# Pooling stage of a hybrid encoder trunk: loads a block ahead, and the next stages' weights in between

## The chip, the cores and the metric

The kernel runs on one core of a Trainium2 chip. Its time is the device time of one execution in microseconds (us); three runs of the kernel before gave 2900.6, 2905.15 and 2907.33 us, median 2905.15. The engines are named as in the profile: PE (TensorE matmul), DVE (VectorE), ACT (ScalarE), POOL (GpSimd), and SP, on which nearly all DMAs of this kernel are issued.

## The reference, cut to what matters

One layer: a combined input projection of x (4096 tokens, width 1024) feeds four mixers of width 256, whose outputs are merged by an output projection.

```python
z = x @ w_in                       # one projection for all four mixers, N_COLS columns
def pool_mix(u, w_grp, scale):     # the mixer of the stage that is changed
    cs = cumsum(u)                 # along the tokens
    means = [(cs[t] - cs[t - win]) / min(t + 1, win) for win in (2, 4, 8, 16)]
    d = concat(means) - u          # 64 columns for each window
    return einsum('bsgc,gcd->bsgd', d, w_grp) * scale   # then gated by silu of a further 256 columns
# retention_mix, mlstm_mix, rwkv7_mix: the stages that follow, each with its columns of w_in
out = layer_norm(alpha * x + concat(mixers) @ w_out + gated_embedding)
```

Products run on operands that are split exactly in two parts (hi, the cast, and lo, the rest), with three matmuls for each pair: hi·hi, hi·lo and lo·hi.

## The kernel before, in words

Tokens are worked on in 16 blocks of 256. The stages follow each other: pooling (`pooling`), retention, the matrix memory (mLSTM), and at last RWKV with the output. `pooling` goes through the blocks: `dense(b)` loads the block's x in four quarters of the contraction (`load_x`, `fetch`: a DMA into a raw tile L83, the cast to hi on ACT L84, the subtraction for lo on DVE L85), then runs 48 matmuls into `zu` (the pooled columns) and 24 for each half of the tokens into `zpg` (the gate, with 8 columns of mLSTM gates). `mix(b - 1)` makes the windows' sums on POOL (`s`, L784 to L789), the differences on DVE (`dp`, L798), a small product on PE (`yp`, L803), and the result `Yp` on DVE and POOL (L805, L806), stored by SP (L729).

In between the stage prepares right operands for the next two stages, which use seven products in place of eight, so that four of their seven weight operands are sums of quarters of the weights. `sums(name, k)` loads four pieces of a row k (L1288) into tiles `w0` to `w3`, makes four subtractions on POOL (L1290) and stores them as `T5`, `T7`, `T6`, `T4` in DRAM (L1291); `right(name, n)` loads an operand (L1310), casts it (L1311) and subtracts (L1312). Each of the four rows of `w_rt` (retention), six operands of retention and four rows of `w_ml` (mLSTM) is one entry of a list; one entry is taken per block, from block 2 on.

What sets the order on the engines: the program is written in this order and then ordered by a scheduler with a simulated time line; an instruction wrapped in `keep_in_program_order` stays in the order of the program among those so wrapped. Every engine, and SP's queue too, runs its instructions in the order they stand in. Buffers are rings: x parts `xh` and `xl` have 5 (`XB`), raw tiles 3 (and up to 12 early loads take a tile of another ring, `spare`), `w0` to `w3` one each. Retention's first tiles are the x quarters `xr` (L1347) and their hi parts `Ah` (L1336); the pools of the pooling stage are closed before, so `xr` may stand where `w0` to `w3` stood.

```python
for _ in range(1 if i < self.NB else len(todo)):
    if todo and i >= 2:
        todo.pop(0)()
```

Of the kernel before, what the change touches and what calls it, by code (L numbers as in the profile page):

```python
# [9 lines left out]
F32 = mybir.dt.float32  # L10
# [7 lines left out]
P = 128  # L18
# [3 lines left out]
XB = 5  # L22
SOON = 800
H = D // 2
PLAIN = 5
# [17 lines left out]
class Trunk:  # L43
# [27 lines left out]
    def fetch(self, hi, lo, src, nm, eng):  # L71
        """load float32 data and split it exactly into hi + lo"""
# [3 lines left out]
        if self.spare % 2:  # L76
            raw = self.zp.tile([P, 2, 15 + TB], F32, name=f"raw{nm}", tag="z2")[:, :, 0:G]
        else:
            raw = self.xp.tile([P, 2, G], F32, name=f"raw{nm}", tag="raw", bufs=3)
# [7 lines left out]
    def weights(self, name, g0, w=G, pool=None, bufs=5, gates=False):  # L87
        """hi and lo parts of columns g0..g0+w of a weight matrix"""
# [6 lines left out]
        def parts():  # L95
            for k in range(0, KT, 2):
                ks = slice(k, k + 2)
                yield self.fetch(hi[:, ks, :w], lo[:, ks, :w], self.a[name][:, ks, g0:g0 + w], f"{name}_{g0}_{k}",
                                 nc.vector if k < 4 else nc.gpsimd)
            if gates:  # L100
                yield self.fetch(hi[:, :, G:], lo[:, :, G:], self.a[name][:, :, g0 + w:g0 + w + 8], f"{name}_g",
                                 nc.gpsimd)
        return (hi, lo), parts()

    def lazy(self, *args, **kw):
        """a weight group that is loaded where it is first used"""
# [11 lines left out]
    def load_x(self, b, more=None, between=None):  # L118
        """the block's tokens in quarters of the contraction; three of eight come from the pool more"""
        his, los = [], []  # L120
        for k in range(0, KT, 2):
            p, n = (more, 3) if more is not None and (4 * b + k // 2) % 8 in (1, 4, 7) else (self.xp, XB)
# [16 lines left out]
    def dense(self, jobs, nk=KT, apart=False):  # L139
        """out = lhsT.T @ rhs for each job; operands are (hi, lo) by contraction tile.  # L140
        The jobs share one bank unless apart and advance together, so one start flag clears it."""
# [7 lines left out]
    def dense_k(self, jobs):  # L149
        """the same in steps of one contraction tile, in this order on the engine"""  # L150
# [8 lines left out]
    def cols(self, z, w, x, n=2):  # L159
        """columns of one weight group on the partitions, tokens along the row"""  # L160
# [3 lines left out]
    def toks(self, jobs, nk=KT, apart=False):  # L164
        """tokens on the partitions: jobs of (out, weights, x, first token)"""
# [4 lines left out]
    def silu_gate(self, sg, z):  # L170
        """twice z * sigmoid(z)"""
# [13 lines left out]
    # ------------------------------------------------------------------ RWKV  # L185
# [6 lines left out]
    def _rwkv_out(self, es):  # L192
# [20 lines left out]
        # low-rank weights: decay rows (hi, lo), rate rows (lo, hi), against twice the upper part of their input  # L213
# [43 lines left out]
        def mixed(b, out, z, c0, n):  # L257
            """z + (previous token's z - z) * mu, by columns"""
# [11 lines left out]
        # what a block goes through, in pieces: generators that yield the time of the products they have issued  # L270
# [53 lines left out]
        def l(b):  # L324
            # low-rank decay and rate
# [32 lines left out]
        def n(b):  # L358
            # squared norm of the removal key, by tokens in the order of the rows of its products
# [11 lines left out]
            # rows (kappa, beta) of an even chunk, (beta, kappa) of an odd one  # L371
# [61 lines left out]
        def s_(b, cc):  # L433
            # token-major copies of (kappa, beta)
# [11 lines left out]
        def p_(b, cc):  # L446
            # scores of the chunk
# [52 lines left out]
        # inverse of I - N, N strictly upper in this layout  # L500
# [23 lines left out]
        def iv(b):  # L524
# [3 lines left out]
            with self.soon():  # L528
                # the four blocks of 4 on the diagonal, row by row from below
# [7 lines left out]
                # pairs of blocks: X12 = X11 (N12 X22), the inner product where N has zeros  # L537
# [25 lines left out]
        def pt(b):  # L563
            # pairs of 16 to blocks of 32: rows and columns of one block of 32, what N has in the pairs meets zeros
# [29 lines left out]
        def pu(b):  # L594
            # blocks of 32 to 64
# [23 lines left out]
        def chain(b):  # L619
            """the four chunks of a block, one after another; yields where their products wait"""  # L620
# [90 lines left out]
    def head_norm(self, pool, Y, eps, nm):  # L711
        """normalise each 64-wide head of Y [P, 2, 256] in place"""
# [18 lines left out]
    # ------------------------------------------------------------------ pooling  # L731
    def pooling(self, es):
# [6 lines left out]
        p2 = pool("p2", bufs=2)  # L739
        self.mm = pool("pmm", bufs=4, space=PSUM)  # L740
# [4 lines left out]
        # the first products wait for these alone  # L745
# [12 lines left out]
        bl = {}  # L758

        def dense(b):  # L760
            x = self.load_x(b) if b else x0
# [13 lines left out]
        def mix(b):  # L775
# [25 lines left out]
            for c in range(2):  # L801
                for i in range(2):
# [7 lines left out]
        todo = [lambda k=k: self.sums(ws, "w_rt", k) for k in range(4)]  # L810
        qpair = lambda nm: [self.aq.tile([P, 4, H], F32R, name=f"{nm}{g}", tag="q") for g in range(2)]
        todo += [lambda n=n: self.rtB.update({n: self.right("w_rt", n, (self.wpair if n in (1, 5, 2, 6) else qpair)(f"rB{n}"),
                                                           lambda nm: ws.tile([P, H], F32, name=nm, tag=f"w{nm[-1]}"))})
                 for n in (1, 5, 2, 6, 4, 7)]
        todo += [lambda k=k: self.sums(ws, "w_ml", k) for k in range(4)]
        for i in range(self.NB + 1):
            if i < self.NB:
                dense(i)
            if i >= 1:
                mix(i - 1)  # L820
            for _ in range(1 if i < self.NB else len(todo)):
                if todo and i >= 2:
                    todo.pop(0)()

    # ------------------------------------------------------------------ retention
# [133 lines left out]
    # ------------------------------------------------------------------ mLSTM  # L959
    def gates(self, cp, es0):  # L960
        """the stabiliser and the decays of every chunk of 128 tokens, rows (chunk, head)"""
# [724 lines left out]
```

## Time and profile before

| | before |
|---|---|
| runs | 2900.6, 2905.15, 2907.33 us |
| profiled execution, first to last instruction | 2898.2 us |
| PE busy | 2773.1 us (96%), 21940 matmuls |
| DVE busy | 2270.0 us (78%) |
| POOL, ACT busy | 1156.9 us (40%), 974.5 us (34%) |
| mean granted TensorE clock | 0.974 of full speed |
| DMA queue q1 | 277.46 MB, 30.5% of 16 engines' span |

The profiled execution is 2898.2 us from its first to its last instruction; the runs, which include what lies around that, are 2.4 to 9.1 us longer. Times in rows are microseconds from the start of the span unless marked ns. A busy PE is not PE at its peak: the ends of matmuls are modelled and overlap. A row of idle time names what ended it.

### The profile page before, as it was taken

To read this page: it belongs to the slowest core of one execution; us is meant where nothing else is said; L and a number is where in the kernel's file an instruction comes from. 1 tells how busy PE (TensorE), PEld (TensorE's weight loads), DVE (VectorE), ACT (ScalarE), POOL (GpSimd) and SP (SyncE) were. 2 spreads that over 40 slices of the span, in tenths; PEclk is the share of its full clock that TensorE was granted. 3 is DMA by queue.
4 is the path that set the end of the run, shared out by engine and by line. 5 is a ranking of instruction groups with operands and counts; after the bars stand their busy time and mean duration, and the time that the engine had idled before them with its cause. 6 is when DMAs were issued, how large, how long until landed. Compare 5 with 4: busy or idle time off the path is not lost.

```text
span 2898.2 us, 57364 instructions
## 1 busy us (share of the span) xinstructions
PE 2773.1 (96%) x21940; PEld 2466.1 (85%) x21940; DVE 2270.0 (78%) x5639; ACT 974.5 (34%) x2100; POOL 1156.9 (40%) x1231
## 2 busy tenths in 40 slices
PE   7899999999999999798999999999999999999997
PEld 7898888878999999688999999998998788777885
DVE  5657788887999999976777777778847566689997
ACT  3423223234433333333333333334423233432221
POOL 6654555553333333421232333223326111156665
PEclk9899999999999999888999999999999999999998
DMA  7743222223211111321111111112437444643441
GB/s 241 218 142 102 59 66 66 63 72 110 71 59 56 59 53 55 103 59 29 47 34 41 44 37 45 34 45 60 133 106 260 149 139 138 221 153 139 148 157 66
DMA packets 250499, 281.13 MB, mean 97 GB/s; under 512 B 69488, under 2 KB 166512, under 8 KB 250224
## 3 DMA queue, kind: packets, MB, share of 16 engines
q1 hardware_dynamic: 250224, 277.46, 30.5%
q8 instruction: 172, 2.82, 0.4%
q14 instruction: 103, 0.84, 0.1%
HBM read 209.69 MB, written 67.70 MB: 96 GB/s over the span
## 4 chain that ended last, share of the span: by engine, by line
PE 41%; DVE 10%; POOL 3%; DMA 2%; issue 2%; ACT 1%; SPq 0%; POOLq 0%; DVEq 0%; ACTq 0%
PE ry L273 3%; PE gp L273 2%; DVE ro L1578 2%; DVE ro L1557 1%; PE sa L273 1%; PE l L273 1%; PE zg L154 1%; DVE ro L1560 1%; PE zpl L147 1%; PE zpl L145 1%; PE zpl L146 1%; PE zg L155 1%; PE zg L156 1%; POOL ro L1561 1%; PE zpe L145 1%
## 5 line engine op out<-in xcount | busy, mean ns | idle before, releaser
L1336 ACT CAST Ah<-xr 128x512 fp32r<-128x512 f32 x189 | 117.0, 620 | 277.7 <-PE zrb L1372 58.7
L1337 DVE TENSOR_TENSOR Al<-xr,Ah 128x512 fp32r<-128x512 f32 x135 | 99.8, 739 | 76.5 <-ACT Ah L1336 75.7
L677 POOL TENSOR_TENSOR SAV<-SAV,bon 64x256 f32<-64x256 f32 x64 | 40.7, 636 | 283.9 <-PE ry L273 282.3
L85 DVE TENSOR_TENSOR xl<-rawx,xh 128x512 fp32r<-128x512 f32 x148 | 120.9, 821 | 39.8 <-ACT xh L84 38.9
L145 PE MATMUL zqk<-xh,wh_w_ml 128*128 128x256 f32 x512 | 149.1, 291 | 1.1 <-ACT xh L1078 1.1
L146 PE MATMUL zqk<-xl,wh_w_ml 128*128 128x256 f32 x512 | 149.1, 291 | 0.3 <-DVE xl L1079 0.3
L147 PE MATMUL zqk<-xh,wl_w_ml 128*128 128x256 f32 x512 | 149.2, 291 | 0.0
L84 ACT CAST xh<-rawx 128x512 fp32r<-128x512 f32 x148 | 91.6, 619 | 168.8 <-DMA rawx<-in_xT 72.3
L1337 POOL TENSOR_TENSOR Al<-xr,Ah 128x512 fp32r<-128x512 f32 x54 | 71.8, 1330 | 135.7 <-ACT Ah L1336 72.2
L1561 POOL TENSOR_TENSOR ro<-ro,ln_b 128x512 f32<-128x512 f32 x64 | 100.6, 1591 | 53.9 <-DVE ro L1560 53.9
L660 DVE SCALAR_TENSOR_TENSOR S<-ds,eC,Se 64x64 f32<-64x64 f32 x256 | 72.5, 283 | 53.4 <-PE ds L273 48.7
L866 POOL TENSOR_TENSOR rot<-rot,sw 128x256 f32<-128x256 f32 x64 | 69.4, 1085 | 94.2 <-DVE sw L865 88.5
L145 PEld LDWEIGHTS zqk<-xh,wh_w_ml 128*128 128x128 f32 x512 | 98.0, 191 | 3.6 <-ACT xh L1078 1.6
L147 PEld LDWEIGHTS zqk<-xh,wl_w_ml 128*128 128x128 f32 x512 | 98.1, 192 | 2.4
L146 PEld LDWEIGHTS zqk<-xl,wh_w_ml 128*128 128x128 f32 x512 | 98.2, 192 | 2.0 <-DVE xl L1079 0.8
L459 DVE SCALAR_TENSOR_TENSOR g<-gp,rc,c_rmask 128x128 f32<-128x128 f32 x256 | 72.1, 343 | 33.9 <-PE gp L273 32.8
L145 PE MATMUL zu<-xh,wh_w_pl 128*128 128x256 f32 x256 | 78.7, 308 | 14.7 <-ACT xh L84 8.9
L1356 POOL TENSOR_TENSOR xr<-xr,xr 128x512 f32<-128x512 f32 x27 | 35.5, 1316 | 141.8 <-DVE xr L1353 141.7
L146 PE MATMUL zu<-xl,wh_w_pl 128*128 128x256 f32 x256 | 78.2, 305 | 12.0 <-DVE xl L85 12.0
L1185 DVE SCALAR_TENSOR_TENSOR xc<-zc,c_convw,xc 128x256 f32<-128x256 f32 x192 | 86.2, 497 | 0.4
L273 PE MATMUL ry<-SAV,g 64*64 64x64 f32 (+1 forms) x1024 | 83.5, 223 | 0.0
L798 DVE SCALAR_TENSOR_TENSOR dp<-s,c_pinv,us 64x256 f32<-64x256 f32 (+1 forms) x64 | 44.5, 695 | 47.9 <-POOL s L784 41.7
(1120 smaller groups left out, 10675.9 us busy)
## 6 DMA issues: line engine op xcount, KB each, us to landing
rawx<-in_xT SPq DMA_DIRECT2D x148, 256.0 KB, 3.3
xr<-in_xT SPq DMA_DIRECT2D x108, 256.0 KB, 2.9
mr<-in_xT SPq DMA_DIRECT2D x64, 256.0 KB, 3.1
rp<-in_x SPq DMA_DIRECT2D x64, 256.0 KB, 3.1
s<-rp SPq DMA_DIRECT2D x64, 256.0 KB, 2.5
yo<-y SPq DMA_DIRECT2D x16, 1024.0 KB, 4.9
ro<-s SPq DMA_DIRECT2D x16, 1024.0 KB, 5.0
out<-ro SPq DMA_DIRECT2D x32, 512.0 KB, 2.6
```

The costliest lines, as they stand in the source:

```text
L84: nc.scalar.copy(out=hi, in_=raw)
L85: eng.tensor_tensor(out=lo, in0=raw, in1=hi.bitcast(F32), op=ALU.subtract)
L145: nc.tensor.matmul(out, lh(k), rh(k), start=(k == 0 and (apart or i == 0)), stop=False, skip_group_check=True)
L146: nc.tensor.matmul(out, lh(k), rl(k), start=False, stop=False, skip_group_check=True)
L147: nc.tensor.matmul(out, ll(k), rh(k), start=False, stop=(k == nk - 1), skip_group_check=True)
L273: mm = lambda *args, **kw: keep(nc.tensor.matmul(*args, **kw))
L459: V.scalar_tensor_tensor(out=g1[cc][:, hh, p, e], in0=gp[hh][:, p, e], scalar=rc[:, cc, e, i:i + 1], in1=msk[:, 64 * e:64 * e + P], op0=AL ...
L660: V.scalar_tensor_tensor(out=Sn[hv, p, hv], in0=ds[hv, p], scalar=eC[hv, p, c:c + 1], in1=Se[hv, p], op0=ALU.mult, op1=ALU.add)
L1185: V.scalar_tensor_tensor(out=xc[:, t], in0=zc[t // 2][:, t % 2, j:j + TB], scalar=cw[:, t, j:j + 1], in1=xc[:, t], op0=ALU.mult, op1=ALU.add)
L1336: self.nc.scalar.copy(out=hi, in_=src)
L1337: eng.tensor_tensor(out=lo, in0=src, in1=hi.bitcast(F32), op=ALU.subtract)
L1561: Q.tensor_tensor(out=rg, in0=rg, in1=ln["ln_b", g], op=ALU.add)
```

## The change

Five things change. In the loop of `pooling`, the loads of block i + 1 are written ahead of `dense(i)` (before: at the start of `dense(b)`). The x parts get two more buffers (pool `px`), so seven quarters in all. The four rows of sums of `w_rt` are written at the ends of blocks 1 to 5, the six operands at blocks 6 to 11, the sums of `w_ml` at blocks 12 to 16; of a row, the loads and subtractions stand at one block and the four stores at the next one, just ahead of the next row's loads. The DMAs of sums and operands, and the operands' casts, are kept in program order. And of the gate weights, the 8 gate columns are loaded first, and all of their lo parts are made on DVE.

```diff
 def fetch(self, hi, lo, src, nm, eng):
-        if self.spare % 2:
+        if self.spare % 2 and list(src.shape) == [P, 2, G]:
...
 def weights(...):
         def parts():
+            if gates:
+                yield self.fetch(hi[:, :, G:], lo[:, :, G:], self.a[name][:, :, g0 + w:g0 + w + 8], f"{name}_g",
+                                 nc.vector)
             for k in range(0, KT, 2):
...
-                                 nc.vector if k < 4 else nc.gpsimd)
-            if gates:
-                yield self.fetch(hi[:, :, G:], lo[:, :, G:], self.a[name][:, :, g0 + w:g0 + w + 8], f"{name}_g",
-                                 nc.gpsimd)
+                                 nc.vector if k < 4 or gates else nc.gpsimd)
...
 def load_x(self, b, more=None, between=None):
-            p, n = (more, 3) if more is not None and (4 * b + k // 2) % 8 in (1, 4, 7) else (self.xp, XB)
+            p, n = (more, 2) if more is not None and (4 * b + k // 2) % 7 in (3, 6) else (self.xp, XB)
...
 def pooling(self, es):
+        px = pool("px", bufs=2)
...
+        xs = {0: x0}
         def dense(b):
-            x = self.load_x(b) if b else x0
+            x = xs.pop(b)
...
-        todo = [lambda k=k: self.sums(ws, "w_rt", k) for k in range(4)]
-        todo += [...the six operands of w_rt, by right()...]
-        todo += [lambda k=k: self.sums(ws, "w_ml", k) for k in range(4)]
+        keep = tc.keep_in_program_order
+        def operand(n):
+            t = (self.wpair if n in (1, 5, 2, 6) else qpair)(f"rB{n}")
+            self.rtB[n] = self.right("w_rt", n, t, lambda nm: ws.tile([P, H], F32, name=nm, tag=f"w{nm[-1]}"), keep)
+        def rows(name):
+            for k in range(4):
+                part = self.sums(ws, name, k, keep=keep)
+                next(part)
+                yield
+                next(part, None)
+        plan = {i: [] for i in range(self.NB + 1)}
+        for i in range(5):
+            plan[1 + i].append("rt")
+            plan[12 + i].append("ml")
+        for i, n in enumerate((1, 5, 2, 6, 4, 7)):
+            plan[6 + i].append(n)
+        row = {nm: rows(f"w_{nm}") for nm in ("rt", "ml")}
         for i in range(self.NB + 1):
+            if i + 1 < self.NB:
+                xs[i + 1] = self.load_x(i + 1, more=px)
             if i < self.NB:
                 dense(i)
             if i >= 1:
                 mix(i - 1)
-            for _ in range(1 if i < self.NB else len(todo)):
-                if todo and i >= 2:
-                    todo.pop(0)()
+            for w in plan[i]:
+                if w in row:
+                    next(row[w], None)
+                else:
+                    operand(w)
...
 def sums(self, ws, name, k, j=0, w=H, keep=lambda i: i):
-            nc.sync.dma_start(out=t[i], in_=self.a[name][:, 4 * kh + k, o:o + n])
+            keep(nc.sync.dma_start(out=t[i], in_=self.a[name][:, 4 * kh + k, o:o + n]))
         for i, o, x, y in ((5, 1, 0, 1), (7, 0, 3, 0), (6, 3, 3, 1), (4, 2, 2, 3)):
             Q.tensor_tensor(out=t[o], in0=t[x], in1=t[y], op=ALU.subtract)
-            nc.sync.dma_start(out=self.T[name][i][:, k, j:j + n], in_=t[o])
+        yield
+        for i, o in ((5, 1), (7, 0), (6, 3), (4, 2)):
+            keep(nc.sync.dma_start(out=self.T[name][i][:, k, j:j + n], in_=t[o]))
```

SP's queue in the middle of the stage, before: `rawx3_0` is the first quarter of block 3's x, `w..._rt30` and `T..._rt` are loads and stores of sums of `w_rt`, `y0` the store of block 0.

```order
L83 DMA rawx3_6_674<-in_xT 128x512
L1288 DMA w0w_rt30_1157<-in_w_rt 128x512
L729 DMA y0_72<-Yp0_475 128x2x256
L1291 DMA T6w_rt_636<-w3w_rt20_984 128x512
L1288 DMA w1w_rt30_1151<-in_w_rt 128x512
L1291 DMA T4w_rt_634<-w2w_rt20_982 128x512
```

And now, at the store of block 1:

```order
L83 DMA rawx5_0_866<-in_xT 128x512
L83 DMA rawx5_2_872<-in_xT 128x512
L729 DMA y1_73<-Yp1_673 128x2x256
L1316 DMA T5w_rt_507<-w1w_rt00_510 128x512
...
L1316 DMA T4w_rt_506<-w2w_rt00_512 128x512
L1311 DMA w1w_rt10_681<-in_w_rt 128x512
```

The store of block 0 stood behind the loads of block 3, that of block 1 now stands behind half of block 5's; the sums' transfers, which stood between single quarters of x, now stand together behind the store of a block.

SP's queue before, where the sums of `w_ml` end and the x of retention's first block (`xr0`) is loaded, amid blocks 9 and 10 of 16:

```order
L1291 DMA T6w_ml_2362<-w3w_ml30_2881 128x384
L1291 DMA T4w_ml_2360<-w2w_ml30_2879 128x384
L83 DMA rawx10_0_1861<-in_xT 128x512
L83 DMA rawx10_2_1867<-in_xT 128x512
L1347 DMA xr0_00_2971<-in_xT 128x4x128
```

And now, behind the stage's last store:

```order
L1316 DMA T4w_ml_2387<-w2w_ml20_2735 128x384
L1311 DMA w1w_ml30_2880<-in_w_ml 128x384
L729 DMA y15_87<-Yp15_2911 128x2x256
L1311 DMA w2w_ml30_2882<-in_w_ml 128x384
...
L1311 DMA w0w_ml30_2886<-in_w_ml 128x384
...
L1316 DMA T5w_ml_2388<-w1w_ml30_2880 128x384
...
L1316 DMA T4w_ml_2387<-w2w_ml30_2882 128x384
L1372 DMA xr0_00_2975<-in_xT 128x4x128
```

The last row of sums, its stores and the load of `xr0` moved from the middle of the stage to behind `y15`.

POOL at the end of the stage, before (`s215` to `s1615` are the windows' sums of block 15, `s2` to `s16`):

```order
L785 TENSOR_TENSOR s415_2895<-s215_2894 128x2x268
L1312 TENSOR_TENSOR rB3wlg_2942<-raww_rt33_2955,rB3whg_2941 128x512
L788 TENSOR_TENSOR s815_2898<-s415_2895 128x264
L1356 TENSOR_TENSOR xr0_10_2975<-xr0_00_2971,xr0_10_2975 128x512
L789 TENSOR_TENSOR s1615_2899<-s815_2898 64x256
L806 TENSOR_TENSOR Yp14_2873<-Yp14_2873,c_pl_scale_200 128x512
```

And now (of the rows up to the last subtraction of the sums):

```order
L787 TENSOR_TENSOR s415_2894<-s215_2893 128x2x268
L1313 TENSOR_TENSOR w1w_ml20_2733<-w0w_ml20_2739,w1w_ml20_2733 128x384
L790 TENSOR_TENSOR s815_2897<-s415_2894 128x264
L1337 TENSOR_TENSOR rB3wlg_2946<-raww_rt33_2959,rB3whg_2945 128x512
L1313 TENSOR_TENSOR w0w_ml20_2739<-w3w_ml20_2737,w0w_ml20_2739 128x384
L791 TENSOR_TENSOR s1615_2898<-s815_2897 64x256
L808 TENSOR_TENSOR Yp14_2872<-Yp14_2872,c_pl_scale_203 128x512
...
L1313 TENSOR_TENSOR w2w_ml20_2735<-w2w_ml20_2735,w3w_ml20_2737 128x384
L808 TENSOR_TENSOR Yp15_2911<-Yp15_2911,c_pl_scale_203 128x512
...
L1313 TENSOR_TENSOR w1w_ml30_2880<-w0w_ml30_2886,w1w_ml30_2880 128x384
...
L1313 TENSOR_TENSOR w2w_ml30_2882<-w2w_ml30_2882,w3w_ml30_2884 128x384
```

Eight subtractions of the sums of `w_ml` now stand among and behind block 15's own work on POOL. On PE, the last `zpg` of block 15 was followed by `yp14`, 24 matmuls of retention and then `yp15`; now it is followed by `yp14`, `yp15` and then retention.

## Rows read from the trace of the kernel before

**Rows 1.** Busy time of the engines by stretch, core 0.

```profile
core 0: us, PE busy (x) PEld busy (x) DVE busy (x) ACT busy (x) POOL busy (x), PEclk, DMA share, GB/s
40.00:169.00 129.00, 108.74 (x830) 106.59 (x829) 83.18 (x124) 42.39 (x81) 85.78 (x81) 0.92 0.73 224
...
181.60:194.03 12.43, 12.43 (x106) 12.43 (x106) 7.22 (x14) 3.83 (x8) 5.35 (x6) 1.00 0.33 107
...
253.00:300.00 47.00, 47.00 (x237) 38.28 (x236) 35.22 (x80) 14.72 (x28) 25.08 (x27) 1.00 0.34 99
```

**Rows 2.** Time line of PE: start, duration, line, operands.

```profile
39.92 0.83 PE L803 MATMUL yp<-c_plw,dp 128*128 128x128 f32 x6
...
243.87 1.28 PE L803 MATMUL yp<-c_plw,dp 128*128 128x128 f32 x10
244.90 0.48 PE L1371 MATMUL zra<-rB1whg,Ah 128*128 128x512 f32 x1
...
249.39 0.50 PE L1373 MATMUL zrc<-rB5whg,Al 128*128 128x512 f32 x1 [1.01 <-DVE Al L1337]
...
252.20 0.94 PE L803 MATMUL yp<-c_plw,dp 128*128 128x128 f32 x6 [0.25 <-DVE dp L798]
```

**Rows 3.** Waits from 40 to 169 us: total, times, longest.

```profile
ACT xh L84 <- DMA rawx<-in_xT: 42.4, 10, 9.8
...
PE zu L146 <- DVE xl L85: 11.6, 7, 3.6
```

**Rows 4.** Busy time by stretch, right after an idle time of PE.

```profile
74.60:79.00 4.40, 3.60 (x15) 3.31 (x16) 4.37 (x6) 2.98 (x6) 1.78 (x2) 0.50 0.68 216
```

**Rows 5.** Time line of ACT: casts of the gate columns and of `xr`.

```profile
18.78 0.24 ACT L84 CAST wh_w_pl<-raww_pl_g 128x64 fp32r<-128x64 f32 x1 [2.77 <-DMA raww_pl_g<-in_w_pl]
...
242.77 0.62 ACT L1336 CAST Ah<-xr 128x512 fp32r<-128x512 f32 x1
```

**Rows 6.** PE, groups up to 244 us: busy, mean ns, idle before.

```profile
L145 PE MATMUL zu<-xh,wh_w_pl 128*128 128x256 f32 x256 | 78.7, 308 | 14.7 <-ACT xh L84 8.9 <-ACT wh_w_pl L84 5.8
...
L145 PE MATMUL zpg<-wh_w_pl,xh 128*128 128x264 f32 x256 | 73.2, 287 | 3.7 <-ACT wh_w_pl L84 3.7
```

**Rows 7.** Time line of POOL at the end of the stage.

```profile
241.13 1.41 POOL L785 TENSOR_TENSOR s<-s 128x536 f32<-128x536 f32 x1
242.94 1.29 POOL L1312 TENSOR_TENSOR rB3wlg<-raww_rt,rB3whg 128x512 fp32r<-128x512 f32 x1 [0.41 <-ACT rB3whg L1311]
244.19 0.81 POOL L788 TENSOR_TENSOR s<-s 128x264 f32<-128x264 f32 x1
...
247.73 1.06 POOL L789 TENSOR_TENSOR s<-s 64x256 f32<-64x256 f32 x1
```

**Rows 8.** POOL, groups up to 260 us: busy, mean ns, idle before.

```profile
L806 POOL TENSOR_TENSOR Yp<-Yp,c_pl_scale 128x512 f32<-128x512 f32 x16 | 22.8, 1424 | 30.4 <-issue 27.6 <-DVE Yp L805 2.5
...
L1290 POOL TENSOR_TENSOR w3w_ml<-w3w_ml,w1w_ml 128x384 f32<-128x384 f32 x4 | 5.3, 1327 | 0.2
...
L1290 POOL TENSOR_TENSOR w1w_ml<-w0w_ml,w1w_ml 128x384 f32<-128x384 f32 x4 | 4.0, 1011 | 8.2 <-DMA w0w_ml<-in_w_ml 2.9 <-issue 2.7 <-DVE xl L85 1.6
```

**Rows 9.** DMA issues from 100 to 170 us: count, KB each, median us to landing.

```profile
w0w_ml<-in_w_ml SPq DMA_DIRECT2D x4, 192.0 KB, 3.6
...
T5w_ml<-w1w_ml SPq DMA_DIRECT2D x4, 192.0 KB, 2.5
```

**Rows 10.** DMA issues from 231 to 262 us.

```profile
xr<-in_xT SPq DMA_DIRECT2D x4, 256.0 KB, 2.9
```

**Rows 11.** POOL's first subtraction of the four rows of `w_ml`: ns min/median/max, first to last start.

```profile
L1290 POOL TENSOR_TENSOR w1w_ml<-w0w_ml,w1w_ml x4: 997/1013/1022, 114.6 to 149.3; 128x384 f32<-128x384 f32 x4
```

**Rows 12.** DVE, groups from 100 to 170 us (first two) and 169 to 231 us (last).

```profile
L798 DVE SCALAR_TENSOR_TENSOR dp<-s,c_pinv,us 64x256 f32<-64x256 f32 x19 | 13.7, 722 | 20.9 <-POOL s L784 18.3 <-POOL s L788 1.7 <-POOL s L789 0.6
L1312 DVE TENSOR_TENSOR rB<-raww_rt,rB 128x512 fp32r<-128x512 f32 x6 | 6.0, 997 | 3.8 <-ACT rB L1311 3.7
...
L798 DVE SCALAR_TENSOR_TENSOR dp<-s,c_pinv,us 64x256 f32<-64x256 f32 x20 | 9.6, 480 | 18.2 <-POOL s L784 17.9
```

More of the change, by code (lines that the diff above doesn't have):

```diff
@@ L809, in pooling @@
         self.rtB = {}
-        todo = [lambda k=k: self.sums(ws, "w_rt", k) for k in range(4)]
+        keep = tc.keep_in_program_order
         qpair = lambda nm: [self.aq.tile([P, 4, H], F32R, name=f"{nm}{g}", tag="q") for g in range(2)]
-        todo += [lambda n=n: self.rtB.update({n: self.right("w_rt", n, (self.wpair if n in (1, 5, 2, 6) else qpair)(f"rB{n}"),
-                                                           lambda nm: ws.tile([P, H], F32, name=nm, tag=f"w{nm[-1]}"))})
-                 for n in (1, 5, 2, 6, 4, 7)]
-        todo += [lambda k=k: self.sums(ws, "w_ml", k) for k in range(4)]
+        def operand(n):
[14 more added lines that the diff above has]
+        row = {nm: rows(f"w_{nm}") for nm in ("rt", "ml")}
         for i in range(self.NB + 1):
+            if i + 1 < self.NB:
+                xs[i + 1] = self.load_x(i + 1, more=px)
             if i < self.NB:
@@ L1275, in half, with sums @@
         return (2 * G, 3 * P) if name == "w_ml" else (0, H)
-    def sums(self, ws, name, k, j=0, w=H):
+    def sums(self, ws, name, k, j=0, w=H, keep=lambda i: i):
         nc, Q = self.nc, self.nc.gpsimd
@@ L1287, in sums, with right @@
             o = c0 + nh * hw + j
-            nc.sync.dma_start(out=t[i], in_=self.a[name][:, 4 * kh + k, o:o + n])
+            keep(nc.sync.dma_start(out=t[i], in_=self.a[name][:, 4 * kh + k, o:o + n]))
         for i, o, x, y in ((5, 1, 0, 1), (7, 0, 3, 0), (6, 3, 3, 1), (4, 2, 2, 3)):
             Q.tensor_tensor(out=t[o], in0=t[x], in1=t[y], op=ALU.subtract)
-            nc.sync.dma_start(out=self.T[name][i][:, k, j:j + n], in_=t[o])
-    def right(self, name, n, tiles, raws=None):
+        yield
+        for i, o in ((5, 1), (7, 0), (6, 3), (4, 2)):
+            keep(nc.sync.dma_start(out=self.T[name][i][:, k, j:j + n], in_=t[o]))
+    def right(self, name, n, tiles, raws=None, keep=lambda i: i):
         nc = self.nc
@@ L1309, in right @@
                     .rearrange("p a b -> p (a b)")[:, :hw]
-            nc.sync.dma_start(out=raw, in_=src)
-            nc.scalar.copy(out=hi[:, k], in_=raw)
+            keep(nc.sync.dma_start(out=raw, in_=src))
+            keep(nc.scalar.copy(out=hi[:, k], in_=raw))
             (nc.gpsimd if k == 3 else nc.vector).tensor_tensor(out=lo[:, k], in0=raw, in1=hi[:, k].bitcast(F32),
@@ L1496, in out @@
             if 0 <= i - PLAIN - 1 < 4:
-                self.sums(ws, "w_out", i - PLAIN - 1)
+                list(self.sums(ws, "w_out", i - PLAIN - 1))
         ln = {}
```

## The prediction, made before the changed kernel ran

> **What bounds the kernel now.** I read the table of busy times first: PE is busy for 96% of the span, so only what frees or idles PE can move the end. The table by stretches says where it idles [rows 1]: in retention it is busy for 47.00 of 47 us at full clock, in one late block of pooling for 12.43 of 12.43 us, but from 40 to 169 us for 108.74 of 129 us at a granted clock of 0.92, while the DMA share is 0.73 against 0.33. So what the change can win lies ahead of 169 us, and the late block shows what a block costs when nothing is missing: 12.43 us.
>
> The time line of PE gives the size [rows 2]. The product `yp` of block 0, which stands behind block 1, is at 39.92 us; block 15's last `zpg` ends at 243.87 us, and retention's first `zra` starts at 244.90. Between lie 14 blocks: 203.95 us, where 14 x 12.43 = 174.0 would do. 29.9 us are lost: 129 - 108.74 = 20.3 us of idle, and 9.6 us more, for which the slower clock is the likely place.
>
> The waits name the cause [rows 3]: ACT's casts `xh` wait 42.4 us for the raw x, ten times, up to 9.8 us, and PE's `zu` waits behind them (11.6 us for `xl`, which comes from the same raw tile). In SP's queue, quarters of x stand between loads and stores of sums, and a store waits there for POOL. The clock follows: in the 4.40 us after one idle time the granted clock is 0.50 [rows 4], the 1.2 GHz level, so about 2.2 us of work are lost again after it.
>
> **The change part by part.** *Loads a block ahead, seven quarters.* The x of block i + 1 is issued before block i is computed, and a store of sums that waits now holds back quarters that PE needs more than a block later. The cast of a quarter waits only until PE has released the one seven before it, so PE has three quarters of a block (over 9 us) in hand, and the longest wait is 9.8. I take 28 of the 29.9 us as won, leaving 2 for that worst one; the low end is 20 (the idle goes, the clock does not), the high end 29.9.
>
> *Gate columns first.* At the start, the cast of the gate columns waits 2.77 us for its DMA [rows 5], part of 3.7 us that the `zpg` wait for weights; PE's first matmul is at 5.8 us, which is the idle before `zu` that ends with `wh_w_pl` [rows 6]. Two whole blocks from there would end at 5.8 + 24.9 = 30.7, not 39.92, so the gain lies between 0 (the weights' quarters now queue for raw tiles with x) and 9.2. I take the 3.7. The lo parts that go from POOL to DVE are three short subtractions; PE waits for nothing of POOL's there, so I give them 0; if DVE holds up `xl` by them they cost about 1 us each, by the `rB` row below. Block 15 so ends 31.7 us earlier, at 212.2.
>
> *The last row of sums and `xr`.* This is the wait that the change adds, and it is certain from the order: the loads, four subtractions and four stores of row 3 of `w_ml` now stand behind block 15, and `xr0` behind these stores in SP's queue. Behind `xr0` wait ACT's cast `Ah`, DVE's `Al`, and all of retention on PE; only `yp14` and `yp15` are left to fill the time. I count from E, the end of block 15's last `zpg` (243.87 before). POOL ended `s16` at 247.73 + 1.06 = E + 4.9 [rows 7]. Two subtractions of row 2 now stand ahead of it, 1.01 and, between 1.01 and 1.33, 1.1 us [rows 8]: E + 7.0. Then `Yp14` 1.42, two more subtractions 1.33 + 1.1: E + 10.9. The store `T4` of row 2 lands 2.5 us after its issue, and the loads of row 3 into the same tiles land 3.6 us later [rows 9]: E + 17.0. On POOL follow four subtractions, 4.5 us, with two small ones between (0.9 by the 0.81 of `s8`): E + 22.4. Then `xr0` is issued and lands 2.9 us later [rows 10], and its cast takes the 0.62 of [rows 5]: `zra` starts at E + 25.9, where it started at E + 1.03. The price is 24.9 us. Low end 18 (transfers of 2.5 us, and POOL with row 2 ahead of its place), high end 29 (5 us for each of the two loads, another wait of a microsecond).
>
> The Trainium skill ("DMA: Bandwidth & Descriptors", section on the anatomy of one DMA, SWDGE path) gives about 2.0 us fixed for a transfer, and bytes / 436e3 on top; it also says that waits on semaphores happen on the issuing sequencer, which is what makes a waiting store hold back `xr0` here. The formula would give an estimate of 2.45 us for a piece of 192 KB and 2.6 us for `xr`, so the gap would be some 1.5 us shorter; the store's 2.5 us agrees, the load's 3.6 does not, and I go by the rows.
>
> *What comes back.* `yp15`, with its wait 0.94 + 0.25, and the 1.01 us that `zrc` waited for `Al` [rows 2] now lie in the gap: 2.2 us. But PE has idled, and by [rows 4] the restart at half clock costs 2.2.
>
> *Sums and operands spread out.* Before, one row of sums took (149.3 - 114.6) / 3 = 11.6 us from one to the next [rows 11], under the 12.43 of a block, and the stores now wait a block longer: I give the spreading 0 in the middle blocks, covered by PE's quarters in hand. On DVE it may cost. In the loaded stretch the `dp` row's mean is 722 ns, in the light one 480, and `rB` takes 997 ns [rows 12]. An operand at each of blocks 6 to 11 brings four `rB`, of which POOL takes some. Busy DVE is then at most 7.22 + 4 x (0.722 - 0.480) + 3 x 0.997 = 11.2 us of 12.43, so it should fit; uncovered it would be the second rival's price.
>
> The `dp` rows differ by half where POOL's load differs. The Trainium skill ("SBUF — State Buffer", section on SBUF's two separate sides) says that DVE and GpSimd share a port pair as an exclusive lock, so that one fully blocks the other. That speaks against spreading POOL's subtractions over all blocks, and feeds the second rival; by it alone the sum would stay, since DVE keeps a microsecond free in a block.
>
> *Sum*: 28 + 3.7 - 24.9 + 2.2 - 2.2 = 6.8 us less. The profiled execution would go from 2898.2 to 2891.4 us. Retention and what follows are PE-bound, so the shift should reach the end. The median stands 6.95 us above that span, and I keep the distance: 2905.15 - 6.8 = 2898.
>
> **The rivals.** *The gap is short and the start full.* If transfers are quick and POOL is ahead, the gap costs 18, and the start gives 9.2: 29.9 + 9.2 - 18 + 0 = 21 us less, 2884. For it: the two medians of [rows 9] differ by 1.1 us under load, and the load is light at E. Against it: POOL's order puts row 2 among `s8` and `s16`, whose time depends on block 15.
>
> *DVE becomes the bound in blocks 6 to 11: slower.* Each `dp` waits for a sum `s` of POOL, 18 to 21 us for about twenty of them [rows 12], about 4 us in a block, in DVE's order, so the `xl` behind it waits too. 11.2 + 4 = 15.2 us against 12.43 gives 2.8 us in each of six blocks, 17 us; the sum becomes 6.8 - 17 = 10 us more, 2915. It decides as soon as busy time and waits on DVE pass 12.43 us in a block. Against it: quarters in hand let DVE work ahead, and most of that wait is idle time in which it had nothing else to do.
>
> *The change does not do what it says.* The loads of sums wait for stores of the row before in SP's queue, a block's x stands behind them, and ACT waits as before. With half of the 28 won: 6.8 - 14 = 7 us more, 2912. Against it: the x is at least a block ahead.
>
> **How the numbers follow.** Chances: the forecast 0.58, short gap and full start 0.12, DVE bound 0.13, no effect on x 0.08, anything else 0.09. The likeliest case alone has a range of 2889 to 2908 (gap 18 to 29, x 20 to 29.9, not all at their ends). About 0.2% (5.8 us) is what a measurement of this kernel tells from no change: faster is below 2899.3, slower above 2911. The forecast lies near the first bound: of its 0.58, 0.34 are faster and 0.24 the same. The first rival is faster, the second and third slower. With the rest split 0.05, 0.04 and 0, that is 0.51 faster, 0.28 the same, 0.21 slower. For 8 in 10 the range goes to 2884 on one side and 2912 on the other.
>
> **What would show it.** In the profile after: no wait of `xh` for raw x above 2 us from 40 to 200 us, and a granted clock near 1 there; block 15's last `zpg` ends near 212 us (207 to 216); then one idle time of PE of 20 to 27 us that ends with ACT's `Ah` and, behind it, the DMA of `xr`, and a granted clock of 0.5 behind it; `zra` at about 238 us. If that idle time is under 15 us, the chain through POOL and SP is wrong; if it is there but `zu` still waits, for `xl` in blocks 6 to 11 or for raw x, the second or third rival holds; if the end of retention is not earlier by what `zra` is, the stage behind was not PE-bound.

## The result and the profile after

The changed kernel is slower: 2931.37 us (median of 4 runs, 2930.74 to 2934.17) against 2903.87 us for the kernel before, a ratio of 1.010 with a 95% interval of 1.0085 to 1.0116. The medians differ by 27.5 us. The profiled execution takes 2929.6 us, 31.4 more than before (the one profiled before was the fastest of its runs). The prediction of 2898 us, and its range of 2884 to 2912, missed.

The busy times by stretch (the same columns as [rows 1]) show where:

```profile
40.00:169.00 129.00, 114.30 (x895) 112.44 (x894) 70.04 (x114) 35.08 (x69) 74.71 (x71) 0.95 0.55 177
169.00:231.50 62.50, 54.56 (x412) 53.56 (x411) 36.47 (x61) 21.95 (x42) 30.16 (x29) 0.92 0.47 139
...
244.00:278.00 34.00, 3.39 (x17) 2.63 (x15) 6.50 (x10) 1.49 (x3) 18.79 (x22) 0.56 0.68 213
278.00:325.00 47.00, 46.92 (x217) 37.94 (x218) 35.81 (x70) 15.26 (x29) 19.39 (x20) 0.95 0.24 69
```

From 40 to 169 us PE is busy for 114.30 us in place of 108.74, so something was won there. But the stretch behind it, in which PE never waited before, now has 8 us of idle time, and 34 us pass behind block 15 with PE almost empty. Retention itself is as dense as it was. PE's time line across that place answers to [rows 2]:

```profile
243.92 1.05 PE L805 MATMUL yp<-c_plw,dp 128*128 128x128 f32 x8
249.69 0.77 PE L805 MATMUL yp<-c_plw,dp 128*128 128x128 f32 x2 [4.72 <-DVE dp L800]
259.74 1.65 PE L805 MATMUL yp<-c_plw,dp 128*128 128x128 f32 x6 [9.28 <-DVE dp L800]
278.08 0.79 PE L1396 MATMUL zra<-rB1whg,Ah 128*128 128x512 f32 x1 [16.69 <-ACT Ah L1361]
```

Block 15 ends at 243.92 us; before, it ended at 243.87. The pooling stage has gained nothing. Retention's first matmul, which stood 1.03 us behind that point, is now 34.2 us behind it: 33.1 us lost, which is the whole difference of the spans but for 1.8 us won back later.

That the blocks come out even hides two changes. The small product `yp` of a block stands behind the next block's matmuls, so the distance of two of them is a block's time. Block 1 ends at 34.11 us, where it ended at 39.92. Then the distances are 12.4 to 12.5 us three times, 14.3, 17.9 and 13.7 (the blocks with rows of `w_rt`, 8.6 us over what three blocks need), 19.7, 16.5, 14.7, 19.3, 14.1 and 17.4 (the blocks with operands, 27.0 us over six blocks), and 12.4 to 12.5 for the last two. Before, the same stretch lost 29.9 us in other blocks; by the same sum (14 blocks of 12.43 us) it now loses 35.8.

**The blocks with rows of `w_rt`.** SP's queue, start and time of the issue:

```profile
72.10 0.38 SPq L729 DMA_DIRECT2D y<-Yp  x1
...
74.71 0.32 SPq L1316 DMA_DIRECT2D T4w_rt<-w2w_rt  x1
76.01 0.33 SPq L1311 DMA_DIRECT2D w1w_rt<-in_w_rt  x1
...
78.81 0.38 SPq L1311 DMA_DIRECT2D w0w_rt<-in_w_rt  x1
79.25 0.42 SPq L83 DMA_DIRECT2D rawx<-in_xT  x1
...
88.59 0.38 SPq L729 DMA_DIRECT2D y<-Yp  x1
```

and POOL's time line beside it:

```profile
84.15 1.29 POOL L1313 TENSOR_TENSOR w1w_rt<-w0w_rt,w1w_rt 128x512 f32<-128x512 f32 x1 [5.06 <-DMA rawx<-in_xT]
85.53 1.78 POOL L1313 TENSOR_TENSOR w0w_rt<-w3w_rt,w0w_rt 128x512 f32<-128x512 f32 x1
87.27 1.29 POOL L808 TENSOR_TENSOR Yp<-Yp,c_pl_scale 128x512 f32<-128x512 f32 x1
```

Read as one chain, this is a circle. The last store of a row, `T4` at 74.71, waits for the row's last subtraction on POOL; the loads of the next row go into the same tiles and wait for the stores to land (the last load is at 78.81), and only then comes x. The loads land, two subtractions run on POOL from 84.15 (the row puts this wait down to x, but what the subtraction reads is `w0` and `w1`), `Yp` stands behind them, and the next `y` is at 88.59. One turn takes 16.5 us.

What PE waits for in these blocks is not the landing of x, though. Lines of POOL, DVE, ACT and PE, in block 6:

```profile
86.10 1.14 ACT L84 CAST xh<-rawx 128x512 fp32r<-128x512 f32 x2
88.52 1.29 POOL L1313 TENSOR_TENSOR w3w_rt<-w3w_rt,w1w_rt 128x512 f32<-128x512 f32 x1
89.89 1.30 POOL L1313 TENSOR_TENSOR w2w_rt<-w2w_rt,w3w_rt 128x512 f32<-128x512 f32 x1
91.15 1.09 POOL L786 TENSOR_TENSOR s<-us 128x540 f32<-128x540 f32 x1
92.27 1.43 DVE L800 SCALAR_TENSOR_TENSOR dp<-s,c_pinv,us 64x256 f32<-64x256 f32 x1 [6.11 <-POOL s L786]
94.03 0.96 DVE L85 TENSOR_TENSOR xl<-rawx,xh 128x512 fp32r<-128x512 f32 x1
95.05 0.58 PE L146 MATMUL zu<-xl,wh_w_pl 128*128 128x256 f32 x1 [3.79 <-DVE xl L85]
```

The block's fourth quarter has landed and is cast at 86.10. Its `xl` runs only at 94.03, since a `dp` stands ahead of it on DVE and waits 6.11 us for the window sum `s`, and `s` stands on POOL behind all four subtractions of the row. PE's stops in blocks 5 and 7 (1.64 and 0.94 us) have the same form; there `dp` waits 4.84 and 4.86 us. So the circle reaches PE through the orders of POOL and DVE. The waits from 40 to 169 us (engine, what waits, for what: total, times, longest) answer to [rows 3]: ACT waits for x no less than it did, but that is not what PE loses.

```profile
ACT xh L84 <- DMA rawx<-in_xT: 54.8, 10, 10.3
...
PE zu L146 <- DVE xl L85: 11.8, 6, 3.8
```

The kernel before already stopped like this, and behind the casts of operands too. Its ACT and DVE time lines, ahead of PE's waits of 5.54 us (to 74.55) and 3.64 us (to 140.75):

```profile
70.29 0.62 ACT L1311 CAST rB1whg<-raww_rt 128x512 fp32r<-128x512 f32 x1 [6.15 <-DMA raww_rt<-in_w_rt]
...
73.88 0.61 ACT L84 CAST xh<-rawx 128x512 fp32r<-128x512 f32 x1
...
132.41 1.34 ACT L84 CAST xh<-rawx 128x512 fp32r<-128x512 f32 x2 [0.22 <-PE zpg L146]
138.81 0.48 DVE L798 SCALAR_TENSOR_TENSOR dp<-s,c_pinv,us 64x256 f32<-64x256 f32 x1 [6.88 <-POOL s L784]
...
139.62 2.56 DVE L85 TENSOR_TENSOR xl<-rawx,xh 128x512 fp32r<-128x512 f32 x2
```

The cast at 73.88 has no wait of its own; it stands behind an operand's casts, which wait for their loads. The `xl` at 139.62 stands behind a `dp`, 7 us after its cast. At every stop of PE's `zu` between 40 and 169 us, in either kernel, the transfer of the quarter that it wants had landed over 4 us before PE ran out.

**The blocks with operands.** ACT's time line:

```profile
113.25 0.62 ACT L84 CAST xh<-rawx 128x512 fp32r<-128x512 f32 x1 [7.28 <-DMA rawx<-in_xT]
113.78 0.58 ACT L767 COPY us<-zu 128x512 f32<-128x512 f32 x1
122.22 1.94 ACT L1336 CAST rB1whg<-raww_rt 128x512 fp32r<-128x512 f32 x3 [7.86 <-DMA raww_rt<-in_w_rt]
...
124.85 1.66 ACT L84 CAST xh<-rawx 128x512 fp32r<-128x512 f32 x3
```

and SP's queue:

```profile
110.12 6.58 SPq L83 DMA_DIRECT2D rawx<-in_xT  x4
116.80 0.39 SPq L729 DMA_DIRECT2D y<-Yp  x1
117.23 2.01 SPq L1335 DMA_DIRECT2D raww_rt<-in_w_rt  x4
127.79 5.52 SPq L83 DMA_DIRECT2D rawx<-in_xT  x4
```

The last three of the four x issued from 110 us on have their casts in ACT's order behind those of the operand, whose loads are issued after them: the fourth x waits for a raw tile, and `y` and the operand's loads stand behind it. ACT stands still for 7.86 us; the three x casts are at 124.85, only then do raw tiles come free, and the next x is issued at 127.79. PE waits 2.79 us for the cast and 1.72 for `xl`. In SP's queue the longest waits of all are those of x for a raw tile, which `xl` sets free (93.8 us from 40 to 244 us, 62.6 before). There are three raw tiles, and no run varied that number.

### The profile page after: what moved, and what is told of

Same layout as the page of the kernel before. It is cut to its first block, busy times and chain, and to the rows that moved or that the text cites. A ratio compares the mean times of both kernels' runs of the same rounds, so it can differ in the third digit from the quotient of the medians.

```text
span 2929.6 us, 57348 instructions
## 1 busy us (share of the span) xinstructions
PE 2778.0 (95%) x21940; PEld 2468.9 (84%) x21940; DVE 2259.9 (77%) x5642; ACT 972.8 (33%) x2100; POOL 1151.9 (39%) x1228
## 5 line engine op out<-in xcount | busy, mean ns | idle before, releaser
L85 DVE TENSOR_TENSOR xl<-rawx,xh 128x512 fp32r<-128x512 f32 x148 | 113.9, 779 | 36.2 <-ACT xh L84 35.3
L146 PE MATMUL zu<-xl,wh_w_pl 128*128 128x256 f32 x256 | 75.9, 296 | 16.7 <-DVE xl L85 16.7
L657 POOL TENSOR_TENSOR Se<-S,eC 64x128 f32<-64x128 f32 x128 | 68.2, 533 | 33.7 <-DVE S L660 29.1
```

The lines of the kernel that those rows point to most:

```text
L85: eng.tensor_tensor(out=lo, in0=raw, in1=hi.bitcast(F32), op=ALU.subtract)
L146: nc.tensor.matmul(out, lh(k), rl(k), start=False, stop=False, skip_group_check=True)
```

## The experiments

| kernel | time, us | before in the same set, us | ratio to before (95%) | block 15 ends, us | first `zra`, us |
|---|---|---|---|---|---|
| before | 2903.87 | | | 243.87 | 244.90 |
| changed | 2931.37 | 2903.87 | 1.0085 to 1.0116 | 243.92 | 278.08 |
| e1_shift | 2922.86 | 2899.64 | 1.0063 to 1.0093 | 244.47 | 268.55 |
| e2_oplate | 2902.68 | 2899.64 | 1.0001 to 1.0020 | 215.59 | 249.19 |
| e4_poolsub | 2926.56 | 2899.64 | 1.0077 to 1.0110 | 238.54 | 271.98 |
| e5_storepool | 2919.56 | 2899.64 | 1.0053 to 1.0094 | 224.66 | 263.05 |
| e6_nokeep | 2888.16 | 2902.04 | 0.9939 to 0.9968 | 238.16 | 239.19 |
| e7_ahead7 | 2894.87 | 2902.04 | 0.9968 to 0.9988 | 240.88 | 241.99 |
| e10_early | 2889.48 | 2902.04 | 0.9942 to 0.9971 | 230.09 | 240.28 |
| e11_early_pool | 2905.38 | 2902.04 | 1.0001 to 1.0021 | 224.93 | 250.40 |
| f1_late_mlfree | 2882.20 | 2900.19 | 0.9925 to 0.9950 | 222.72 | 230.58 |
| f2_early_mlfree | 2884.48 | 2900.19 | 0.9931 to 0.9958 | 228.56 | 231.76 |
| f3_late_mlfree_ypool | 2881.95 | 2899.77 | 0.9920 to 0.9947 | 218.04 | 227.11 |
| f4_mlfree_ypool | 2884.07 | 2899.77 | 0.9931 to 0.9955 | 216.10 | 232.61 |

The kernel before ran anew in each set of runs, and its median moved by up to 4 us. So a time is compared with one of another set only to within some 4 us; the ratios are within their sets.

My theory after the result: three losses of one kind, an instruction in an in-order queue that waits for something issued too late, with everything behind it. The rivals: DVE is the bound where PE waits for `xl`, or the DMA traffic itself.

**e2_oplate: the casts of an operand a block behind its loads.**

```
 def operand(n):
+    raws = [ws.tile(...) for k in range(4)]
+    self.right("w_rt", n, t, raws, keep, casts=False)   # the loads
+    yield
     self.rtB[n] = self.right("w_rt", n, t, raws, keep)  # casts and lo parts, one block later
```

> The changed kernel with the casts and lo parts of an operand written one block behind its loads. Theory of the order on ACT (the operand's casts stand ahead of the next block's last x quarter and wait 6 to 8 us for a load issued behind the store y): these waits vanish, the seven blocks from 104 to 219 us, which took 115 us, take under 95, and the time falls by about 20 us to 2911. Rival, that DVE is the bound there (zu waits 16.7 us for xl): the same work is on DVE, the waits stay, 2931 within 4. Rival, that the DMA traffic itself is the bound: the same bytes, 2931 within 4.

All six operand blocks take 12.4 to 12.5 us; block 15 ends at 215.59, 28.3 us earlier than in the changed kernel. The time falls by 28.7 us (some 26 by the ratios), to 0.1% over the kernel before. The same bytes move and DVE has the same work, so both rivals fall for these blocks. The gap behind block 15 stays, at 33.6 us. ACT's time line, the same operand:

```profile
118.82 0.38 ACT L173 ACTIVATE spg<-zpg 128x256 f32<-128x256 f32 x1
120.69 2.63 ACT L1349 CAST rB1whg<-raww_rt 128x512 fp32r<-128x512 f32 x4 [1.50 <-DMA raww_rt<-in_w_rt]
124.75 0.62 ACT L84 CAST xh<-rawx 128x512 fp32r<-128x512 f32 x1 [1.43 <-DMA rawx<-in_xT]
...
126.38 1.34 ACT L84 CAST xh<-rawx 128x512 fp32r<-128x512 f32 x2 [0.21 <-PE zpg L146]
```

The casts wait 1.50 us in place of 7.86. With them, the lo parts on DVE and POOL moved back too; which of the three engines' orders did most is not separated. The last row shows one thing more: the casts of a block's next quarters are released by PE's `zpg`, 2.1 us ahead of the end of the block before (128.48).

**e4_poolsub: the rival of DVE, by itself.**

```
-(nc.gpsimd if k == 3 else nc.vector).tensor_tensor(out=lo[:, k], ...)
+(nc.gpsimd if k == 3 or raws else nc.vector).tensor_tensor(out=lo[:, k], ...)
```

> The changed kernel with all lo parts of the six operands made on POOL (three of four were on DVE). Theory that DVE bounds the operand blocks: three subtractions of about 1 us leave DVE in each of six blocks, zu no longer waits for xl there, some 15 us less, 2916. Theory of the order on ACT and SP: nothing gained, and POOL has 3 x 1.3 us more in a block ahead of its window sums, so 2931 to 2940.

With DVE relieved of three subtractions in a block, the operand blocks take 18.9, 16.7, 13.4, 17.6, 17.0 and 12.5 us: five of six are still long. The waits from 104 to 219 us in this kernel show that only the engine named has changed:

```profile
ACT rB1whg L1336 <- DMA raww_rt<-in_w_rt: 9.1, 2, 8.4
...
PE zu L145 <- ACT xh L84: 7.8, 4, 4.1
```

DVE's work is not the bound of these blocks. The 5 us that block 15 comes earlier are a small share of the 27, and the time, 4.8 us less (2 by the ratios), is within what two sets differ by.

**e1_shift: everything behind the sums of `w_rt` a block earlier.**

```
-plan[12 + i].append("ml")
+plan[11 + i].append("ml")
-plan[6 + i].append(n)
+plan[5 + i].append(n)
```

> The changed kernel with the operands one block earlier (blocks 5 to 10) and the sums of w_ml one block earlier (11 to 15), so that the last row's loads and subtractions lie in block 14 and 15. Theory of the chain behind block 15 (the last row of sums, its stores, then xr): the idle time of PE before zra falls from 33.1 us to about 8, the time from 2931 to about 2906 (2900 to 2912), while the blocks before 219 us cost what they cost now. Rival, that xr itself is late for another reason (its memory, or POOL's own work at the end): the gap stays above 25 us and the time near 2931.

The gap falls from 34.2 to 24.1 us, not to 8, and the time by 8.5 us (some 6 by the ratios), not 25. The direction fits the sums of `w_ml`; this run, which moves the operands too, doesn't settle it (e6 and f1 do, below). One block is too little: the rows run late, the last row's first subtraction is still 9 us behind block 15 (253.47 us), and `xr` still stands behind it and behind `y15`.

**e5_storepool: the stores of `y` and of the sums issued by POOL.**

```
-keep(nc.sync.dma_start(out=self.T[name][i][...], in_=t[o]))     # and self.store for y
+keep(nc.gpsimd.dma_start(out=self.T[name][i][...], in_=t[o]))
```

> The changed kernel with the stores of y and of the sums issued by POOL in place of SP. Theory of the loop through SP (the x loads and the next row's loads stand behind stores that wait for POOL): blocks 2 to 5, about 16.5 us each, come down to 13 to 14, and the operand's loads start earlier, together 12 us less, 2919; if POOL's own issuing costs over a microsecond for each store, half of it is given back. Rivals of DVE or of the DMA traffic: 2931 within 4.

The three blocks that took 14.3, 17.9 and 13.7 us take 12.5, 14.1 and 12.5, and those with operands are shorter too: block 15 ends 19.3 us earlier. The time falls by 11.8 us (some 8 by the ratios) where 12 were expected. In POOL's order the window sum `s` now stands ahead of the row's last two subtractions, and `dp` hardly waits:

```profile
72.02 1.52 POOL L787 TENSOR_TENSOR s<-us 128x540 f32<-128x540 f32 x1
73.65 1.28 POOL L1314 TENSOR_TENSOR w3w_rt<-w3w_rt,w1w_rt 128x512 f32<-128x512 f32 x1
...
73.57 1.75 DVE L801 SCALAR_TENSOR_TENSOR dp<-s,c_pinv,us 64x256 f32<-64x256 f32 x1 [0.57 <-POOL s L787]
```

This fits the circle: without it the blocks are short. It does not show that the stores' place in SP's queue is the cause, since the scheduler changed POOL's order with it, and a row's loads still wait in SP's queue for the stores to land. The gap behind block 15 grows by 4 us, to 38.4, and part of the gain is given back there.

**e7_ahead7: loads a block ahead and seven quarters, put into the kernel before.**

```
+if i + 1 < self.NB:
+    xs[i + 1] = self.load_x(i + 1, more=px)
 if i < self.NB:
     dense(i)                       # the list of sums and operands as before, nothing pinned
```

> The kernel before with two parts of the change alone: loads written a block ahead and seven quarters; gate columns, list of sums and operands, and no pins, as before. The prediction gave these two 28 us: 2905 - 28 = about 2875. Theory of the order (x quarters all stay in use until the last quarter of a block, so that seven of them hide only some 4.7 us, and SP's queue stays mixed): a gain under 12 us, 2893 or above, with several zu waits left between 50 and 160 us.

2894.87 us, a ratio of 0.9978 (0.9968 to 0.9988): some 6 us faster, and block 15 ends 3 us earlier. From block 1's end to block 15's, where I had put 28 us, 26.3 us are still lost where 29.9 were: the term is worth 3.6 us there.

**e6_nokeep: the changed kernel with nothing pinned.**

```
-keep = tc.keep_in_program_order
+keep = lambda i: i
```

> The changed kernel with nothing pinned: DMAs and casts of sums and operands are free for the scheduler, the rest as changed. Theory that the pinned places make the losses (operand casts ahead of x casts, the last row behind block 15): the gap before zra falls under 10 us, since the last rows can move forward as they did before, and the time to about 2905 or below. Rival, that the places come from the list by blocks and not from the pins: the order, the gap of 33 us and the time near 2931 stay.

2888.16 us: some 43 us faster than with the pins, and 0.46% (0.32 to 0.61) faster than before. The rows of `w_ml` move forward as they did, and `zra` follows block 15 by 1.03 us. So the pins cost what the rest of the change would win; between 78 and 169 us several blocks still take 14 to 21 us, as they did before.

**e10_early and e11_early_pool: late casts, and everything early.** Rows of `w_rt` from block 0, operands from 4, rows of `w_ml` from 10; e11 adds POOL's stores.

```
-plan[1 + i].append("rt")     # 12 + i: "ml", 6 + i: operand n
+plan[i].append("rt")         # 10 + i: "ml", 4 + i: operand n, casts at 5 + i
```

> The changed kernel with an operand's casts a block behind its loads, and everything earlier: rows of w_rt from block 0, operands from block 4, rows of w_ml from block 10, so that the last stores stand in block 14 and xr in SP's queue ahead of the last two y. Theory of the two orders: block 15 ends near 216 us, as with the late casts alone, and the gap before zra is under 6 us in place of 33; 2903 - 28 = about 2875. Rival, that the gap comes from POOL's windows' sums and the small products of block 15 and not from the sums of w_ml: the gap stays above 20 us, 2895.

> The same with the stores of y and of the sums issued by POOL. Theory of the loop through SP's queue: the two blocks that take 14.2 and 18.3 us at the end of the sums of w_rt come down to about 12.5, some 6 us less than without, 2869. Rival, that POOL's issuing costs as much at its place: no difference or a few us more, 2875 to 2882.

e10 gives 2889.48 us, 13 us under e2 (16 by the ratios) where 28 were expected. Block 15 ends at 230, not 216: two blocks with `w_rt` take 17.7 and 19.6 us, and one with `w_ml` takes 17.6. In each of them PE waits for an `xl` behind a `dp`, which waits 3.6 to 4.9 us for POOL's `s`: the circle came along with the rows. The gap is 10 us, not under 6, and it ends with `yp15`, which waits 8.72 us for `dp`; for this rest of the gap the rival named before the run, POOL's window sums and the small products, is the right one. In e11 most blocks up to 127 us take 12.4 to 12.5 us, but one takes 18.0 (`yp` waits 3.78 us there for `dp`), later ones 18.4 and 15.1, and the gap is 25.5: 2905.38, a miss of 36 us. There the last row is again behind block 15: its first subtraction is at 234.71, 9.8 us behind the block's end, and `xr` is issued at 246.19.

**f1 to f4: late casts, and the rows of `w_ml` not pinned.** f1 also has operands and `w_ml` a block earlier, f2 has them as e10; f3 is f1 with `y` stored by POOL, f4 the same without the block earlier.

```
-part = self.sums(ws, name, k, keep=keep)
+part = self.sums(ws, name, k, keep=keep if name == "w_rt" else (lambda i: i))
```

> The changed kernel with three edits together: an operand's casts a block behind its loads, operands and rows of w_ml a block earlier, and the transfers of w_ml not pinned (those of w_rt and of the operands still are). By the theory of the two orders each repairs its own part: the operand blocks take 12.5 us as with the late casts alone, and the free w_ml rows let xr stand ahead of y15 in SP's queue. Block 15 ends between 216 and 224 us (the rows of w_ml may cost the blocks with x loads 5 us or so), the gap is under 6 us, the time 2872 to 2880. Rival, that the sums of w_ml cost the same wherever they lie: what the gap loses, the blocks take, 2889 as with everything early.

> The same with the rows of w_rt from block 0, operands from block 4 and w_ml from block 10, the transfers of w_ml not pinned. With everything pinned at these places it was 2889, 10 us of gap and two blocks of about 18 us at the rows of w_rt. Theory: the gap goes, the two blocks stay (they come from the pinned chain y, stores, loads, subtractions), 2878 to 2884. Rival, that the sums cost the same wherever they lie: 2889.

> As the kernel at 2882 (late casts, operands and rows of w_ml a block earlier, w_ml not pinned), with one edit more: the store of y is issued by POOL, so that no load in SP's queue stands behind a wait for Yp. Theory of the chain y, stores, loads, subtractions, Yp: the four blocks at 14.0 to 16.2 us (71 to 132 us) come to 13 or less, 8 to 10 us less, and 2873. Rival, that the T stores' landing before the next row's loads is the longest part: under 3 us gained, 2880; POOL's own issuing may cost some of it.

> The same with operands and rows of w_ml in the blocks of the changed kernel (6 to 11, 12 to 16), so one block later. Theory: block 15 ends near 213 us (the rows of w_ml come when hardly any x is left to load), and the last row of sums still stands behind it for part of its length, a gap of 10 to 16 us, so 2876 to 2880. Rival, that the gap stays at 25 us or more since row 3 still waits for row 2 as before: 2890.

f1 beats both kernels: 2882.20 us, 0.62% (0.50 to 0.75) faster than before and 49 us faster than the changed one. SP's queue at the end of the stage, with block 15 ending at 222.72:

```profile
220.83 0.32 SPq L1324 DMA_DIRECT2D T4w_ml<-w2w_ml  x1
222.26 0.37 SPq L729 DMA_DIRECT2D y<-Yp  x1
222.73 2.12 SPq L1385 DMA_DIRECT2D xr<-in_xT  x4
```

The last `T4` is issued at 220.83 where it was at 273.50, and `xr` follows at once. The gap is 7.9 us and the time 2.2 us over what I expected at most. What ends the gap is no longer `xr`: the first two products of `yp15` wait 6.39 us for `dp`, and `zra` stands right behind them. f2 is at 2884.48, half a microsecond over its range, where the rival of "the same cost wherever they lie" would have 2889; its gap is 3 us. f3 shows the circle through `y` again: the blocks at 14.0, 14.3 and 15.9 us in f1 are 13.6, 12.5 and 12.4, and block 15 ends 4.7 us earlier, half of what I expected; the block at 16.2 stays. But the time, 2881.95, is that of f1, and not 2873: by time the rival, that the landing of the `T` stores is the longest part (2880), is the nearer one. `yp15` holds the gap 1.2 us longer, and the 3.5 us by which `zra` is still earlier than in f1 are lost behind the pooling stage (2.9 are left at the last `py`, near 2100 us, 0.9 at the first `t`, near 2240); why is not shown. f4 ends block 15 at 216.10 and pays 16.5 us of gap, 2884.07, half a microsecond over what was expected of the gap and 4 us over the time.

## Why the prediction was wrong

**Loads a block ahead: the step that failed first.** "The waits name the cause": ACT's casts wait for the raw x, "and PE's `zu` waits behind them". From this came "I take 28 of the 29.9 us". The trace after shows 35.8 us lost where 2 should be left, and e7 shows that the two parts by themselves win 3.6 us there. The step took the longest wait in a table for PE's. Where PE did stop, x had landed, and its cast or its `xl` stood behind another instruction that waited, an operand's cast on ACT or a `dp` on DVE. Loading x earlier leaves that as it is. The cover was sized wrongly as well. "PE has three quarters of a block (over 9 us) in hand" counts a quarter of x as a quarter of the block, but a block's `zu` needs all four in its first half, and `zpg` uses all four again until late in the second (the cast at 126.38 in e2 is released by `zpg`). So three quarters in hand cover three quarters of `zu`, about 4.7 us by half of 12.43, and PE's stops in the changed kernel are all at the fourth quarter.

**Operands: priced at nothing but DVE.** I weighed the six operands by DVE's busy time, and found room. There was room: e2 has the same work at 12.4 us a block. What I did not cost is the added wait: casts pinned ahead of x casts on ACT, for loads that are issued behind that x and `y`. It cost 27 us, and e2 won it back. The second rival named the right blocks with the wrong mechanism, and e4 rules out DVE's work as the bound. The rule of the Trainium skill on the shared port pair ("SBUF — State Buffer", section on SBUF's two separate sides), which I set beside it, decides nothing here: from 100 to 170 us `dp` took 694 ns, 722 before, and what delays `xl` is the wait of `dp` for `s`, 4.84 to 6.11 us, and not its length.

**Rows of sums: "I give the spreading 0".** That came from 11.6 us from row to row in [rows 11], under 12.43. But that row shows a free order. With stores and loads pinned between `y` and x, a turn takes 16.5 us; the window sums stand in it, and `dp` and `xl` behind them. ACT does wait for x as the third rival had it (54.8 us), but PE's stops have the form that the second rival gave for the blocks with operands: `xl` behind a `dp` that waits for `s`. I had set against it that "most of that wait is idle time in which it had nothing else to do"; `xl` was there to do, but behind it in the order.

**The gap: the mechanism right, the size short.** The chain through POOL, SP, `xr` and `Ah` is the one forecast, at 24.9 us; it cost 33.1. The part from the store `T4` of row 2 on was right: forecast from E + 10.9 to E + 25.9, 15.0 us, measured from 261.65 to 278.08, 16.4. The rest was short, because I took row 2's loads to have landed about when block 15 ends, which the blocks before did not allow:

```profile
246.17 0.36 SPq L1316 DMA_DIRECT2D T4w_ml<-w2w_ml  x1
...
249.36 0.38 SPq L1311 DMA_DIRECT2D w0w_ml<-in_w_ml  x1
...
261.65 0.32 SPq L1316 DMA_DIRECT2D T4w_ml<-w2w_ml  x1
...
273.50 0.32 SPq L1316 DMA_DIRECT2D T4w_ml<-w2w_ml  x1
273.91 10.24 SPq L1372 DMA_DIRECT2D xr<-in_xT  x5
```

The first of these is row 1's last store, 2.3 us behind block 15; row 2's last load is at 249.36, and its first subtraction at 253.33, 9.4 us behind block 15, with the window sums `s8` and `s16` of block 15 behind it. That is also why `yp15` was late.

**The small terms** held: the start gave 5.8 us (3.7 forecast, 9.2 the upper end), the restart behind the gap is at the 1.2 GHz level as [rows 4] had it (the clock granted from 278.10 to 282.50 us is 0.50), and retention carries the shift to the end within 2 us.

So of the sum's terms, the 28 was a loss of 5.9 (35.8 against 29.9), and the 24.9 was 33.1; the start was 2.1 better, and 1.8 us came back behind `zra`, where the sum had set 2.2 against 2.2.

## What to carry to other kernels

An instruction that is pinned into an in-order queue must be placed where its input has landed, not where its input is issued: moving a consumer a block behind its load added no work and gave 26 to 29 us. A long wait in a table is not yet a loss: begin with what the bounding engine waits for, and look at what stood ahead of that on its own engine. Before giving a spreading a price of nothing, write one turn of the circle down (store, landing, load, work, next store, across all queues) and compare it with a block's time; a free order's pace says nothing of a pinned one's. And buffers in hand are counted by when the last of them is needed and the first comes free, not by their number.

## What the runs showed of the hardware

POOL pays for a DMA it issues: in f3, the 13 stores of `y` from 40 to 212 us take it 764 ns each, where SP's issue of `y` takes 0.38 us in the changed kernel. The columns are busy, mean ns and idle before:

```profile
L730 POOL DMA_DIRECT2D y<-Yp x13 | 9.9, 764 | 0.3 <-POOL Yp L809 0.3
```
